# A hybrid decoder layer on one core: mixers and attention of different quarters alternate piece by piece, and the gate and value products of the last pair are taken in turn

## The chip, the cores and the metric

The kernel runs on one core of a Trainium2 chip. The metric is device time in microseconds from launch to end, lower is better; the time before is the median of three runs. Work is spread over TensorE (PE, matrix products and transposes into PSUM), VectorE (DVE), ScalarE (ACT) and the DMA queue that SyncE (SP) issues. GpSimd (POOL) makes an identity matrix and nothing else.

## The reference

One layer with 2048 tokens of width 1024, in float32:

```python
h = rms_norm(x, mix_norm_g)
lru_x, lru_gate, conf_a, conf_b = split(h @ w_in, 4)           # 512 columns each
lru_x = causal_dwconv(lru_x, lru_conv_w, lru_conv_b)           # 4 taps
y_lru = rg_lru(lru_x, ...) * gelu(lru_gate)                    # two 64x64 gates a head, a scan over time
c = causal_dwconv(conf_a * sigmoid(conf_b), conf_conv_w, ...)  # 31 taps
c = silu(layer_norm(c, ...))
x = x + concat([y_lru, c]) @ w_out
q = rms_norm(x) @ w_q;  k, v = split(rms_norm(mem) @ w_kv, 2)  # 256 memory tokens, 4 heads
x = x + softmax(q k^T / 16) v @ w_o
g, u = split(rms_norm(x) @ w_up, 2)                            # 3072 columns each
x = x + (gelu(causal_dwconv(g, 3 taps)) * u) @ w_down
return rms_norm(x, final_norm_g)
```

## The kernel before

**Arithmetic.** Each matrix product is made of three matmuls: both operands are split into a rounded high part and a low part (`split`: ScalarE copies the high part, VectorE subtracts it), and high x high, high x low and low x high are summed in PSUM (`mm3`). A weight of the mixers that was split once is kept in device memory (`Kept`) and is fetched in two parts for the other three quarters. The memory side of the attention is folded into two matrices of 1024 x 1024 beforehand: `memory_a` makes A (q and k together), `memory_vo` makes VO (v and w_o).

**Stages.** Tokens come in four quarters of 512. For each quarter q there are three tasks. `mixer(q)` (tasks `m`): norm, transpose, then `conf` (two steps, each a projection pair for conf_b and conf_a, followed by 31 taps of convolution on VectorE for two blocks) and `lru` (two steps, each a projection, 4 taps, two gates, a scan, another projection). A mixer starts when the mixer before it has ended. `normed(q)` (tasks `n`): the layer norm of the convolved half, with two column sums on TensorE. `attend(q)` (tasks `a`): `project_tokens` three times (w_out, A, VO) with transposes and a softmax between them, then the norm for the feed-forward, transposed and stored. `project` and `project_tokens` give way (`yield`) after every 12 matmuls. `first_tokens` is the first quarter's own beginning, with the first weight columns.

The feed-forward (`up`) has two halves of 1024 tokens (h = 0, 1). It goes through 12 pairs of column blocks (j); each pair has a gate product and a value product, each by Strassen's scheme with seven products of half size (`strassen_cols`). The operands of x that these need (`HalfX`: seven keys, four tiles each, high and low) stay in SBUF for a whole half: five keys of the first half are made early (`first_x`), two in the first pair. During the value product of the last pair, `used(key)` makes the second half's operand as soon as the first half's has been read. `prepare_down` makes and stores the operands of the down projection in the background. `Down` then does the down projection in three chunks for each half, and `finish` the last norm.

**Order.** The program is written as tasks (generators). `drive` keeps a clock that is the sum of TensorE's planned work; it steps the first task in the list that is due, and `yield n` makes a task due n us later on that clock (`yield task` waits for another task's end). Where none is due the clock jumps, so a wait only orders, it puts no idle time into the program. The list's order is `TURNS`. Every operation recorded this way gets a due time from its place in the order; a planner then simulates the engines, with list scheduling by due times, slots of SBUF tiles (84 of tag S of 512 columns, 4 of tag W for raw weights, 3 of tag D) and 8 PSUM banks, three passes over, and writes out the instructions in the order of the best pass. Each engine then works through its own list in order. All instructions are issued from one helper, so nearly all have line 393 in the profile; one goes by tile names: `conv` are the taps of the long convolution, `xc` those of the short one, `xh`/`xl` high and low parts of mixer inputs and gates' inputs, `yh` of the mixers' results, `xah` and `pth` operands of attention, `Xh` and `wh` the feed-forward's, `hidh` the down projection's.

The constants that set the order stand together:

```python
    EARLY, VO_WAIT, V_LATE, Z_COPIED = 5, 0, 500, ()
    MIX_WAIT, MIX_TURN, LN_SUM, LN_SQ, GATES = (0, 0, 0, 0), 8, 2, 6, 5
    MEM_WAIT, VO_LATE, ATT_TURN, FFN_TURN, X_PACE, T_PACE = 2, 0, 2, 6, 20, 10
    NORMED = [lambda: ([m[0]], 40), lambda: ([attended[0]], 90), lambda: ([attended[1]], 90), lambda: ([m[3], n[2]], 55)]
    TURNS = lambda: [later, m[0], mem_a, m[1], n[0], a[0], mem_vo, n[1], m[2], a[1], n[2], m[3], n[3], first_t, first, a[2], a[3], tail]
```

By tile names the profile shows TensorE in the first mixer to about 121 us, in `memory_a` to 178, in the second mixer to 297, in attention 0 (with the rest of `memory_vo`) to 472, in the third mixer to 571, in attention 1 to 716, in the fourth mixer to 817, in attentions 2 and 3 to 1106, in the first half of `up` to about 1570, the second to about 2010, and in the down projection to the end.

Of the kernel before, what the change touches and what calls it, by code (L numbers as in the profile page):

```python
# [17 lines left out]
P = 128  # L18
# [112 lines left out]
class Program:  # L131
# [68 lines left out]

    def dma(self, out, in_, reads=(), writes=(), join=False):
# [8 lines left out]
        o.store = bool(rd)  # L210
        self.touch(o, rd + list(reads), wr + list(writes), join)
# [21 lines left out]
    def deadlines(self, order):  # L233

        t = 0.0
        for o in self.ops:
            o.due, o.start, o.at = 1e9, None, 0.0
        for o in order:
            if o.eng == "PE":
                o.due = o.turn = t  # L240
                t += o.cost
            elif o.store:
                o.due = t + 30
# [173 lines left out]
def hybrid_layer(  # L417
# [41 lines left out]
    def ps():  # L459
        return pr.new("ps", name="ps")  # L460
# [170 lines left out]
    class Columns:  # L631


        def __init__(self, w, name, n, uses):
            self.w, self.kept, self.uses = w, Kept(name, n * 4) if uses > 1 else None, uses
            self.seen = {}

        def get(self, c0, kq):
            key = (c0, kq)
            n = self.seen[key] = self.seen.get(key, 0) + 1  # L640
            base = ((c0 // (2 * P)) * 2 + kq) * 4
            if n > 1:
                return [tuple(self.kept.get(base + 2 * f + i, (P, KQ, P), "w" + "hl"[i]) for i in range(2)) for f in range(2)]
            got = self.rounded(c0, kq, self.fetch(c0, kq))
            if n < self.uses:
                self.store(c0, kq, got)
            return got
# [34 lines left out]

    def project(W, c0, X):
        pp = [ps(), ps()]
        for kq in range(2):
            ww = W.get(c0, kq)
            for f in range(2):
                wh, wl = ww[f]
                with together():
                    for k in range(KQ):  # L690
                        x = X[kq * KQ + k]
                        mm3(pp[f][:], wh[:, k, :], wl[:, k, :], x[0][:], x[1][:], kq + k == 0, kq == 1 and k == KQ - 1)
                if kq + f < 2:
                    yield 0
        return pp


    def project_tokens(L, W, done, rest=None):

        for half in range(2):  # L700
            pt = [ps() for _ in range(NTB)]
            for k2 in range(NK // 2):
                if rest and half == 0 and k2 == NK // 4:
                    rest()
                ww = [W.get(2 * k2 + j, half) for j in range(2)]
# [58 lines left out]

    def conf(X, C, pb, row):
        for c in (0, 2):
            if pb is None:
                pb = yield from project(W_in, 3 * DL + c * P, X)
            sg = []
# [5 lines left out]
            yield 0  # L775
            pa = yield from project(W_in, 2 * DL + c * P, X)
            cbs = []
# [45 lines left out]

    def lru(q, X, L, row):
        for c in (0, 2):
            pz = yield from project(W_in, c * P, X)
            H = []
            for j in range(2):
                w = vec["v512"][:, c + j, :]
                zt = ztail[c + j]  # L830
                xc, z = tmp("xc"), scaled("z", pz[j], row)
                ACT(xc[:], z[:], AF.Identity, scale=w[:, I_LCW + 3 : I_LCW + 4], bias=w[:, I_LCB : I_LCB + 1])
                if q in Z_COPIED:
                    z = tmp("z")
                    ACT(z[:], pz[j][:], AF.Copy)
                for s in range(1, LK):
                    wt = w[:, I_LCW + 3 - s : I_LCW + 4 - s]
                    V("scalar_tensor_tensor", xc[:, s:], z[:, : TT - s], wt, xc[:, s:], op0=ALU.mult, op1=ALU.add)
                    V("scalar_tensor_tensor", xc[:, :s], zt[:, LK - 1 - s :], wt, xc[:, :s], op0=ALU.mult, op1=ALU.add)
                V("tensor_copy", zt[:], z[:, TT - LK + 1 :])  # L840
                H.append(xc)
            yield GATES
            for j in range(2):
# [26 lines left out]
                H[j] = r  # L870
            pg = yield from project(W_in, DL + c * P, X)
            for j in range(2):
# [181 lines left out]
    def mixer(q, after):  # L1054
        if after:
            yield after
            yield MIX_WAIT[q]
        if q == 0:
            X, pb, row = yield from first_tokens()
        else:  # L1060
            X, pb, row = (yield from mix_norm(q)), None, None
        C, L = [], []
        yield from conf(X, C, pb, row)
        yield from lru(q, X, L, row)
        del X, row
        mixed[q] = C, L

    def first_tokens():
# [100 lines left out]
    def attend(q, ready):  # L1169
# [10 lines left out]

        yield from project_tokens(L + Y, W_out, add)
        del L, Y
# [18 lines left out]

        yield from project_tokens(X, A_rows, soft)
        del X
# [10 lines left out]

        yield from project_tokens(PT, VO_rows, add2, lambda: turn_p(prob[1], PT))
        attended[q].done = True
# [10 lines left out]
        del xs  # L1227
        yield FFN_TURN

# [131 lines left out]
    def up(h, B, used=None):  # L1361
        for j in range(NCH):
            gb = []

# [8 lines left out]

            yield from strassen_cols(2 * j * P, B, gate)
            cvs = []
            for i in range(2):
# [9 lines left out]
            gb = None  # L1386

            def gated(f, th, a, p):
                t = tmp("up")
                V("tensor_tensor", t[:], a[:], p[:], op=ALU.add)  # L1390
                o = th * TT
                V("tensor_tensor", cvs[f][:, o : o + TT], cvs[f][:, o : o + TT], t[:], op=ALU.mult)
# [13 lines left out]
    def wd_at(c, key, i):  # L1406
        return ((c * 7 + ORDER.index(key)) * KD + i) * 2

    def prepare_down():
# [124 lines left out]
    def finish(h, acc):  # L1534
# [45 lines left out]
    NORMED = [lambda: ([m[0]], 40), lambda: ([attended[0]], 90), lambda: ([attended[1]], 90), lambda: ([m[3], n[2]], 55)]  # L1580
    ATTEND = [lambda: [n[0]], lambda: [n[1]], lambda: [n[2]], lambda: [n[3], attended[2]]]
    TURNS = lambda: [later, m[0], mem_a, m[1], n[0], a[0], mem_vo, n[1], m[2], a[1], n[2], m[3], n[3], first_t, first, a[2], a[3], tail]
    X = [HalfX(h) for h in range(NH)]
# [69 lines left out]
```

## Time and profile before

| | |
|---|---|
| median of three runs | 2496.95 us (2496.62 to 2499.46) |
| the profiled execution | 2498.48 us |
| its span, first to last instruction | 2496.7 us |
| TensorE busy, matmuls | 2466.2 us (99%), 11212 |
| VectorE busy, instructions | 1821.8 us (73%), 3041 |
| ScalarE busy, instructions | 1172.3 us (47%), 2039 |
| moved by DMA | 543.70 MB, 218 GB/s |
| mean granted TensorE clock | 0.995 |

A matmul's own duration on record is longer than the distance to the next one, since matmuls overlap; where TensorE loses time is read from idle time in short stretches, from the number of matmuls in them and from the granted clock. In the answers by stretch each row has, behind the length, busy time and (x) instructions of each engine, then the granted clock as a share of full speed, the share of the DMA engines' time, and GB/s.

### The profile page before, as it was taken

To read this page: it belongs to the slowest core of one execution; us is meant where nothing else is said; L and a number is where in the kernel's file an instruction comes from. 1 tells how busy PE (TensorE), PEld (TensorE's weight loads), DVE (VectorE), ACT (ScalarE), POOL (GpSimd) and SP (SyncE) were. 2 spreads that over 40 slices of the span, in tenths; PEclk is the share of its full clock that TensorE was granted. 3 is DMA by queue.
4 is the path that set the end of the run, shared out by engine and by line. 5 is a ranking of instruction groups with operands and counts; after the bars stand their busy time and mean duration, and the time that the engine had idled before them with its cause. 6 is when DMAs were issued, how large, how long until landed. Compare 5 with 4: busy or idle time off the path is not lost. (4 is left out here: it accounts for less than half of the span.)

```text
span 2496.7 us, 32736 instructions
## 1 busy us (share of the span) xinstructions
PE 2466.2 (99%) x11212; PEld 2042.8 (82%) x11212; DVE 1821.8 (73%) x3041; ACT 1172.3 (47%) x2039; POOL 0.7 (0%) x6
## 2 busy tenths in 40 slices
PE   9999999999999999999999999999999999999998
PEld 7897788887888788888888888788888888888887
DVE  6999974199329962339888787987866775667666
ACT  6671846336544653446455455654543432224223
POOL 0000000000000000000000000000000000000000
PEclk9999999999999999999999999999999999999999
DMA  8687676848463788557654545655422288779775
GB/s 311 208 287 267 214 262 226 317 141 298 158 243 115 245 300 316 185 194 261 237 196 149 183 161 186 237 166 181 142 75 93 69 285 284 254 237 341 257 253 177
DMA packets 327742, 543.70 MB, mean 218 GB/s; under 512 B 31581, under 2 KB 109405, under 8 KB 327575
## 3 DMA queue, kind: packets, MB, share of 16 engines
q1 hardware_dynamic: 327574, 541.60, 63.1%
q8 instruction: 89, 1.46, 0.2%
q14 instruction: 79, 0.64, 0.1%
HBM read 396.78 MB, written 144.70 MB: 217 GB/s over the span
## 5 line engine op out<-in xcount | busy, mean ns | idle before, releaser
L393 PE MATMUL ps<-Xh,wl 128*128 128x512 f32 x1344 | 523.6, 390 | 2.7 <-DVE wl L393 2.7
L393 PE MATMUL ps<-Xh,wh 128*128 128x512 f32 x1344 | 523.6, 390 | 1.8 <-ACT u L393 1.1
L393 PE MATMUL ps<-Xl,wh 128*128 128x512 f32 x1344 | 522.9, 389 | 0.0
L393 DVE SCALAR_TENSOR_TENSOR conv<-cb,v,conv 128x512 f32<-128x512 f32 x480 | 334.7, 745 | 1.9 <-ACT conv L393 1.3
L393 PEld LDWEIGHTS ps<-Xh,wl 128*128 128x128 f32 x1344 | 252.2, 188 | 57.7 <-DVE wl L393 5.3
L393 PEld LDWEIGHTS ps<-Xh,wh 128*128 128x128 f32 x1344 | 252.3, 188 | 55.9 <-ACT wh L393 1.9
L393 PEld LDWEIGHTS ps<-Xl,wh 128*128 128x128 f32 x1344 | 252.3, 188 | 52.1
L393 PE MATMUL ps<-wh,hidl 128*128 128x512 f32 x672 | 261.5, 389 | 0.4 <-DVE hidl L393 0.4
L393 PE MATMUL ps<-wh,hidh 128*128 128x512 f32 x672 | 261.5, 389 | 0.0
L393 PE MATMUL ps<-wl,hidh 128*128 128x512 f32 x672 | 261.4, 389 | 0.0
L393 DVE TENSOR_TENSOR acc<-acc,ps 128x512 f32<-128x512 f32 x192 | 129.6, 685 | 147.0 <-PE ps L393 146.5
L393 PE MATMUL ps<-xh,wh 128*128 128x512 f32 x512 | 202.7, 396 | 2.0 <-ACT xh L393 2.0
L393 PE MATMUL ps<-xl,wh 128*128 128x512 f32 x512 | 200.5, 392 | 0.3 <-DVE xl L393 0.3
L393 PE MATMUL ps<-xh,wl 128*128 128x512 f32 x512 | 200.4, 391 | 0.0
L393 ACT ACTIVATE wh<-s 128x512 fp32r<-128x512 f32 x192 | 119.6, 628 | 133.5 <-DVE s L393 98.4
L393 DVE TENSOR_TENSOR wl<-raw,wh 128x512 fp32r<-128x512 f32 x208 | 140.6, 684 | 40.5 <-ACT wh L393 33.8
L393 ACT ACTIVATE wh<-raw 128x512 fp32r<-128x512 f32 x208 | 126.9, 628 | 79.3 <-PE ps L393 43.1
L393 DVE TENSOR_TENSOR wl<-s,wh 128x512 fp32r<-128x512 f32 x192 | 131.2, 686 | 45.1 <-ACT wh L393 30.7
L393 ACT ACTIVATE u<-ps 128x512 f32<-128x512 f32 x144 | 85.9, 597 | 144.3 <-PE ps L393 142.6
L393 PEld LDWEIGHTS ps<-wh,hidh 128*128 128x128 f32 x672 | 126.1, 188 | 26.8 <-ACT hidh L393 0.4
L393 PEld LDWEIGHTS ps<-wh,hidl 128*128 128x128 f32 x672 | 126.1, 188 | 26.7 <-DVE hidl L393 0.8
L393 PEld LDWEIGHTS ps<-wl,hidh 128*128 128x128 f32 x672 | 126.2, 188 | 26.2
(205 smaller groups left out, 4264.4 us busy)
## 6 DMA issues: line engine op xcount, KB each, us to landing
raw<-in_w_up_dram SPq DMA_DIRECT2D x96, 512.0 KB
wh<-w_down SPq DMA_DIRECT2D x164, 256.0 KB
wl<-w_down SPq DMA_DIRECT2D x164, 256.0 KB
wh<-w_in SPq DMA_DIRECT2D x96, 256.0 KB
wl<-w_in SPq DMA_DIRECT2D x96, 256.0 KB
hid<-cv SPq DMA_DIRECT2D x48, 512.0 KB
h<-hid SPq DMA_DIRECT2D x96, 256.0 KB
w_down<-wh SPq DMA_DIRECT2D x84, 256.0 KB
```

What stands on the lines that cost most here:

```text
L393: getattr(e, name)(*[resolve(a) for a in args], **{k: resolve(a) for k, a in kw.items()})
```

## The change

Pieces of a mixer give way for `MIX_PACE[q]` us of the planned clock, and pieces of the three products of an attention for `ATT_PACE[q]`, where both gave way for 0 before. `TURNS`, the waits of `normed` and most other constants are different; `FFN_TURN` has a value for each quarter. In the last pair of each half of `up` the gate's and value's seven products are stepped in turn, and the value's results are held until the gate's are ready. `prepare_down` stops while the first half is in its last two pairs and the second in its first. `first_tokens` fetches both halves of the weight columns at 2*DL (conf_a) right behind those at 3*DL, ahead of the small vectors of `setup_later`. In the second quarter `lru` copies z out of PSUM by ScalarE before the taps. `finish` of the first half multiplies in place. (`dma` gains a parameter whose default is the constant used before.)

```diff
-    def project(W, c0, X):
+    def project(W, c0, X, pace=0):
...
                 if kq + f < 2:
-                    yield 0
+                    yield pace
...
-    def project_tokens(L, W, done, rest=None):
+    def project_tokens(L, W, done, rest=None, pace=0):
...
                     if tb % 2 and k2 < NK // 2 - 1:
-                        yield 0
+                        yield pace
...
-            got = self.rounded(c0, kq, self.fetch(c0, kq))
+            st = self.early.pop(key, None) or raw_cols(self.w, c0, kq)
+            got = self.rounded(c0, kq, st)
...
-                if q in Z_COPIED:
+                if row is None and q in Z_COPIED:
                     z = tmp("z")
                     ACT(z[:], pz[j][:], AF.Copy)
...
             raw.append(W_in.fetch(3 * DL, half))
+        for kq in range(2):
+            W_in.early[2 * DL, kq] = raw_cols(w_in[0], 2 * DL, kq)
...
-        yield from project_tokens(L + Y, W_out, add)
+        yield from project_tokens(L + Y, W_out, add, None, ATT_PACE[q][0])
...
-        yield FFN_TURN
+        yield FFN_TURN[q]
...
-            yield from strassen_cols(2 * j * P, B, gate)
-            cvs = []
+            def gated(f, th, a, p):
+                t = tmp("up")
+                V("tensor_tensor", t[:], a[:], p[:], op=ALU.add)
+                held.append((f, th * TT, t))
+                if cvs:
+                    multiply()
+            def multiply():
+                for f, o, t in held:
+                    V("tensor_tensor", cvs[f][:, o : o + TT], cvs[f][:, o : o + TT], t[:], op=ALU.mult)
+                held.clear()
+            parts = [strassen_cols(2 * j * P, B, gate), strassen_cols(DFF + 2 * j * P, B, gated, used if j == NCH - 1 else None)]
+            turning.done = j >= NCH - PAUSE
+            turned_over.done = h > 0 and j >= 1
+            if used and j == NCH - 1:
+                for _ in zip(*parts):
+                    yield 0
+            yield from parts[0]
...
-            yield from strassen_cols(DFF + 2 * j * P, B, gated, used if j == NCH - 1 else None)
+            multiply()
+            yield from parts[1]
...
     def prepare_down():
         yield attends[NQ - 1]
         for c in range(NCK):
             for i in range(KD):
+                if turning.done:
+                    yield turned_over
...
-                early = tmp("fin")
+                early = tmp("fin") if h else acc[th, tb, 0]
...
-    EARLY, VO_WAIT, V_LATE, Z_COPIED = 5, 0, 500, ()
-    MIX_WAIT, MIX_TURN, LN_SUM, LN_SQ, GATES = (0, 0, 0, 0), 8, 2, 6, 5
-    MEM_WAIT, VO_LATE, ATT_TURN, FFN_TURN, X_PACE, T_PACE = 2, 0, 2, 6, 20, 10
+    EARLY, VO_WAIT, V_LATE, Z_COPIED = 5, 2, 500, (0, 1)
+    MIX_WAIT, MIX_TURN, LN_SUM, LN_SQ, GATES = (0, 10, 0, 0), 9, 2, 0, 4
+    MIX_PACE, ATT_PACE = (1, 4, 4, 4), ((0, 4, 1), (0, 2, 6), (0, 1, 0), (0, 2, 4))
+    PAUSE = 2
+    MEM_WAIT, VO_LATE, ATT_TURN, FFN_TURN, X_PACE, T_PACE = 12, 10, 1, (6, 16, 6, 100), 10, 11
...
+    NORMED = [lambda: ([m[0]], 105), lambda: ([attended[0]], 35), lambda: ([attended[1]], 140), lambda: ([m[3], n[2]], 115)]
+    TURNS = lambda: [later, n[2], m[0], mem_a, m[1], n[1], n[3], a[0], n[0], mem_vo, m[2], first, a[3], a[2], a[1], m[3], first_t, tail]
```

More of the change, by code (lines that the diff above doesn't have):

```diff
@@ L199, in do, with dma @@
         self.touch(o, [r.buf for r in ins] + list(reads), [r.buf for r in outs] + list(writes))
-    def dma(self, out, in_, reads=(), writes=(), join=False):
+    def dma(self, out, in_, reads=(), writes=(), join=False, slack=30):
         o = self.op("SP")
@@ L209, in dma @@
         wr = [out.buf] if isinstance(out, Ref) else []
-        o.store = bool(rd)
+        o.store = slack if rd else False
         self.touch(o, rd + list(reads), wr + list(writes), join)
@@ L242, in deadlines @@
             elif o.store:
-                o.due = t + 30
+                o.due = t + o.store
         for o in reversed(self.ops):
@@ L635, in __init__ @@
             self.w, self.kept, self.uses = w, Kept(name, n * 4) if uses > 1 else None, uses
-            self.seen = {}
+            self.seen, self.early = {}, {}
         def get(self, c0, kq):
@@ L763, in scaled, with conf @@
         return t
-    def conf(X, C, pb, row):
+    def conf(X, C, pb, row, pace):
         for c in (0, 2):
             if pb is None:
-                pb = yield from project(W_in, 3 * DL + c * P, X)
+                pb = yield from project(W_in, 3 * DL + c * P, X, pace)
             sg = []
@@ L775, in conf @@
             yield 0
-            pa = yield from project(W_in, 2 * DL + c * P, X)
+            pa = yield from project(W_in, 2 * DL + c * P, X, pace)
             cbs = []
@@ L822, in conf_out, with lru @@
             Y.append((hi, lo))
-    def lru(q, X, L, row):
+    def lru(q, X, L, row, pace):
         for c in (0, 2):
-            pz = yield from project(W_in, c * P, X)
+            pz = yield from project(W_in, c * P, X, pace)
             H = []
@@ L870, in lru @@
                 H[j] = r
-            pg = yield from project(W_in, DL + c * P, X)
+            pg = yield from project(W_in, DL + c * P, X, pace)
             for j in range(2):
@@ L1062, in mixer @@
         C, L = [], []
-        yield from conf(X, C, pb, row)
-        yield from lru(q, X, L, row)
+        yield from conf(X, C, pb, row, MIX_PACE[q])
+        yield from lru(q, X, L, row, MIX_PACE[q])
         del X, row
@@ L1200, in soft @@
             prob[half].append(softmax(p, rp[:, tb : tb + 1], rn[:, tb : tb + 1]))
-        yield from project_tokens(X, A_rows, soft)
+        yield from project_tokens(X, A_rows, soft, None, ATT_PACE[q][1])
         del X
@@ L1213, in add2 @@
             x2_kept.put((q * NTB + tb) * 2 + half, xs[tb][half][:])
-        yield from project_tokens(PT, VO_rows, add2, lambda: turn_p(prob[1], PT))
+        yield from project_tokens(PT, VO_rows, add2, lambda: turn_p(prob[1], PT), ATT_PACE[q][2])
         attended[q].done = True
@@ L1362, in up @@
         for j in range(NCH):
-            gb = []
+            gb, cvs, held = [], [], []
             def gate(f, th, a, p):
@@ L1386, in up @@
             gb = None
[L1388 to L1392, printed above, removed]
-            yield from strassen_cols(DFF + 2 * j * P, B, gated, used if j == NCH - 1 else None)
+            multiply()
+            yield from parts[1]
             for i in range(2):
@@ L1407, in wd_at @@
         return ((c * 7 + ORDER.index(key)) * KD + i) * 2
+    turning, turned_over = Task(None), Task(None)
     def prepare_down():
@@ L1574, in setup_later @@
         vec["v3072"] = columns([ffn_conv_w[0], ffn_conv_b], DFF, "v3072")
-    EARLY, VO_WAIT, V_LATE, Z_COPIED = 5, 0, 500, ()
-    MIX_WAIT, MIX_TURN, LN_SUM, LN_SQ, GATES = (0, 0, 0, 0), 8, 2, 6, 5
-    MEM_WAIT, VO_LATE, ATT_TURN, FFN_TURN, X_PACE, T_PACE = 2, 0, 2, 6, 20, 10
-    NORMED = [lambda: ([m[0]], 40), lambda: ([attended[0]], 90), lambda: ([attended[1]], 90), lambda: ([m[3], n[2]], 55)]
+    EARLY, VO_WAIT, V_LATE, Z_COPIED = 5, 2, 500, (0, 1)
[4 more added lines that the diff above has]
+    NORMED = [lambda: ([m[0]], 105), lambda: ([attended[0]], 35), lambda: ([attended[1]], 140), lambda: ([m[3], n[2]], 115)]
     ATTEND = [lambda: [n[0]], lambda: [n[1]], lambda: [n[2]], lambda: [n[3], attended[2]]]
-    TURNS = lambda: [later, m[0], mem_a, m[1], n[0], a[0], mem_vo, n[1], m[2], a[1], n[2], m[3], n[3], first_t, first, a[2], a[3], tail]
+    TURNS = lambda: [later, n[2], m[0], mem_a, m[1], n[1], n[3], a[0], n[0], mem_vo, m[2], first, a[3], a[2], a[1], m[3], first_t, tail]
     X = [HalfX(h) for h in range(NH)]
```

## The prediction

> **What bounds the kernel now.** I read the busy line of the page first, then the costliest groups of TensorE, then busy times by stretch with cuts at the stretches where TensorE stops, then the waits and the timeline inside these.
>
> ```profile
> PE 2466.2 (99%) x11212; PEld 2042.8 (82%) x11212; DVE 1821.8 (73%) x3041; ACT 1172.3 (47%) x2039; POOL 0.7 (0%) x6
> ...
> L393 PE MATMUL ps<-Xl,wh 128*128 128x512 f32 x1344 | 522.9, 389 | 0.0
> ```
>
> ```profile
> core 0: us, PE busy (x) PEld busy (x) DVE busy (x) ACT busy (x) POOL busy (x), PEclk, DMA share, GB/s
> 0.00:30.00 30.00, 24.30 (x129) 21.18 (x130) 13.90 (x36) 17.15 (x37) 0.70 (x6) 0.94 0.69 230
> 30.00:180.00 150.00, 150.00 (x809) 130.62 (x808) 146.70 (x273) 104.69 (x182) 0.00 (x0) 1.00 0.80 272
> 180.00:240.00 60.00, 59.67 (x273) 49.10 (x272) 59.50 (x95) 12.77 (x19) 0.00 (x0) 1.00 0.89 308
> 240.00:260.00 20.00, 15.11 (x53) 11.49 (x52) 20.00 (x39) 12.16 (x18) 0.00 (x0) 0.83 0.28 102
> 260.00:290.00 30.00, 30.00 (x133) 24.86 (x132) 28.82 (x56) 19.46 (x28) 0.00 (x0) 1.00 0.44 148
> 290.00:300.00 10.00, 8.91 (x38) 6.70 (x37) 10.00 (x16) 9.90 (x15) 0.00 (x0) 1.00 0.88 305
> 300.00:560.00 260.00, 259.72 (x1226) 216.55 (x1227) 162.16 (x285) 127.03 (x245) 0.00 (x0) 1.00 0.69 243
> 560.00:600.00 40.00, 36.99 (x152) 28.79 (x151) 40.00 (x65) 31.54 (x41) 0.00 (x0) 0.96 0.85 303
> 600.00:800.00 200.00, 199.82 (x943) 166.38 (x942) 114.31 (x206) 89.68 (x183) 0.00 (x0) 1.00 0.55 189
> 800.00:850.00 50.00, 47.03 (x189) 36.85 (x188) 49.28 (x79) 34.29 (x45) 0.00 (x0) 0.93 0.73 259
> 850.00:1105.00 255.00, 254.79 (x1199) 211.62 (x1198) 118.55 (x217) 109.42 (x250) 0.00 (x0) 1.00 0.70 240
> 1105.00:1140.00 35.00, 33.17 (x161) 26.98 (x160) 24.92 (x43) 27.35 (x51) 0.00 (x0) 1.00 0.84 299
> 1140.00:1555.00 415.00, 415.00 (x1833) 343.63 (x1832) 350.41 (x560) 210.32 (x320) 0.00 (x0) 1.00 0.56 188
> 1555.00:1585.00 30.00, 27.35 (x114) 20.47 (x113) 29.54 (x47) 23.68 (x41) 0.00 (x0) 1.00 0.85 287
> 1585.00:2010.00 425.00, 425.00 (x1876) 351.89 (x1875) 327.99 (x499) 196.77 (x297) 0.00 (x0) 1.00 0.39 131
> ...
> 2290.00:2300.00 10.00, 9.58 (x42) 7.29 (x41) 8.91 (x15) 3.72 (x6) 0.00 (x0) 1.00 1.05 389
> ...
> 2490.00:2497.00 7.00, 0.00 (x0) 0.00 (x0) 2.40 (x6) 2.26 (x6) 0.00 (x0) 0.78 0.53 199
> ```
>
> TensorE sets the time. One matmul is on record for 389 ns, but in 1140 to 1555 there are 1833 of them in 415 us: one starts every 226.4 ns, so they overlap, and that spacing is the pace to beat. The change removes no matmul. All it can win is the time in which TensorE stops or runs at a lowered clock. I price a stretch as its length less busy time, plus length times the missing share of the clock: 0 to 30 loses 5.7 + 1.8 = 7.5 us; 240 to 260 loses 4.9 + 3.4 = 8.3; 290 to 300, 1.1; 560 to 600, 3.0 + 1.6 = 4.6; 800 to 850, 3.0 + 3.5 = 6.5; the rest of 180 to 1105 about 1.0 together; 2290 to 2300, 0.4; the end 6.7. In the long runs of equal matmuls I go by the count instead: 1555 to 1585 holds 114 where 30 us at 226.4 ns hold 132.5, so 18.5 x 0.2264 = 4.2 us are lost; 1105 to 1140 by busy time 1.8, and about 2.3 when a matmul that waits overlaps its neighbour as there. Together 42.6 us, and that is the ceiling.
>
> A busy share would hide part of this. The Trainium skill, in "Perfetto Trace Analysis", section Identifying the Most-Contended Engine, calls matmul busy time a poor measure of the distance to roofline because matmuls are pipelined. The rows bear it out: busy time gives 30 - 27.35 = 2.65 us for 1555 to 1585, the count 4.2; by busy time alone my sum below would be some 1.5 us smaller.
>
> Where TensorE stops between 240 and 850, VectorE is full: 58.8 of 60 us in 240 to 300, 40.0 of 40 in 560 to 600, 49.3 of 50 in 800 to 850. Between these it is at 62%, 57% and 46%. The mixers bring VectorE more than TensorE leaves time for, attention less, and the kernel runs them one after the other.
>
> ```profile
> L393 DVE SCALAR_TENSOR_TENSOR conv<-cb,v,conv 128x512 f32<-128x512 f32 x480 | 334.7, 745 | 1.9 <-ACT conv L393 1.3
> ...
> 240.40 0.74 DVE L393 SCALAR_TENSOR_TENSOR xc<-ps,v,xc 128x511 f32<-128x511 f32 x1
> 241.06 0.73 DVE L393 SCALAR_TENSOR_TENSOR conv<-cb,v,conv 128x512 f32<-128x512 f32 x1
> ...
> 246.99 0.73 DVE L393 SCALAR_TENSOR_TENSOR xc<-ps,v,xc 128x509 f32<-128x509 f32 x1
> ...
> 247.83 0.74 PE L393 MATMUL ps<-xh,gwah 128*128 128x512 f32 x1 [4.43 <-ACT xh L393]
> ```
>
> The last four lines show one such stop: VectorE works through the short convolution (xc) that the gates need in turn with taps of the long one (conv), and the gate matmul starts 4.43 us late.
>
> **The change part by part, by the places where time is lost.**
>
> *Start.* Both halves of the second weight column are now fetched ahead of the small vectors.
>
> ```profile
> 3.41 0.98 PE L393 MATMUL ps<-ident,raw 4*128 4x4 f32 x8 [3.41 <-DMA raw<-in_ffn_norm_g_dram]
> ...
> 7.45 0.58 SPq L393 DMA_DIRECT2D raw<-in_conf_conv_w_dram  x1
> ...
> 16.63 0.22 SPq L393 DMA_DIRECT2D raw<-in_conf_ln_b_dram  x1
> ...
> 18.48 0.56 SPq L393 DMA_DIRECT2D raw<-in_w_in_dram  x1
> ...
> 22.77 0.63 ACT L393 ACTIVATE wh<-raw 128x512 fp32r<-128x512 f32 x1 [4.13 <-DMA raw<-in_w_in_dram]
> ...
> 39.69 0.82 ACT L393 ACTIVATE conv<-cb,v 128x512 f32<-128x512 f32 x1 [1.84 <-DVE cb L393]
> ```
>
> The weight is issued at 18.48 behind the vectors (7.45 to 16.63) and the gate matrices, ScalarE stands 4.13 us for it, and the splits of x that TensorE needs are queued behind that instruction. Issued near 7.5 it lands by 12 (18.48 to 22.77 is 4.3 us). Of the 7.5 us, 3.4 precede the first matmul and stay; I take 3.5 of the other 4.1. Late next are the vectors: they need a slot of tag W (four), free when the first column has been split, near 12, then some 9 us on SP's queue (7.45 to 16.63), so they are there by about 24; their first user is at 39.69, 15 us of cover. Bounds: 0 to 4.1 won.
>
> *Mixers against attention.* What is moved is order: each projection piece of 12 matmuls (2.7 us) gives way for 1 us (first quarter) or 4 us, and attention's loops give way in turn; with the new order of tasks the memory's products alternate with the first mixer, `memory_vo` with the second, attention 0 with the end of the second and the third, attention 1 with the fourth. Instructions and transfers on SP stay as many; they come in another order. VectorE in 30 to 1105 sums to 749 us of 1075, 70%; conv alone is 334.7/4 = 84 us in a quarter. A mixer holds 8 x 48 + 48 matmuls, 98 us of TensorE, and an estimated 130 of VectorE (conv, and what the 146.7 us in 30 to 180 hold beside it). An attention holds 3 x 192 and 96 transposes, some 141 us; a stretch of nothing else shows VectorE at 24%, so 34 us:
>
> ```profile
> 650.00:700.00 50.00, 49.82 (x234) 41.05 (x233) 11.95 (x25) 16.90 (x46) 0.00 (x0) 1.00 0.48 170
> ```
>
> Mixed, 164 us of VectorE stand against 239, 69%. So the stops at 560 to 600 and 800 to 850 (11.1 us) should nearly go: 2 left, for the chain of the layer norm. In 30 to 300 two mixers still come early and VectorE stays full (265.0 us of 270 by its five rows); only `memory_vo` moves ahead as filler, and the first attention's output projection comes beside the second mixer's end. Of 9.4 us I leave 4. Small ones stay at 1.0. Won: 21.5 - 7 = 14.5. Bounds: 21.5 won, all of it; the other end is below nothing, the third rival. I sit nearer the gain because the rows just named leave VectorE 38 to 54% idle beside each stop.
>
> *The clock.* Half of the 240 stop's price is the clock (0.83 of 20 us); it goes with the wait. The 1.1 us stop at 290 kept 1.00.
>
> *Entry to the feed-forward.* The last quarter's 32 transposes and eight ScalarE copies wait 100 us instead of 6, and x is prepared at pace 10 instead of 20, ahead of attention 2 and 3. Of 2.3 us I leave 1.3, won 1.0; bounds 0 and 2.3. With these the weights' preparation for the down projection starts 100 us later and pauses over the last two pairs and the first of the second half (3 x 38 us). It is paced (84 steps of 8 us), so it ends near 2005 instead of 1800; its last third is not read before about 2150. VectorE has 97 us free in 1585 to 2010 for it. Cost 0, up to 2 if it collides with the start of the down products.
>
> *Last pair.* Gate and value products alternate, so each operand of x is used twice before its successor is split.
>
> ```profile
> L393 DVE TENSOR_TENSOR wl<-s,wh 128x512 fp32r<-128x512 f32 x192 | 131.2, 686 | 45.1 <-ACT wh L393 30.7 <-PE ps L393 13.1
> L393 DVE SCALAR_TENSOR_TENSOR cv<-gb,v,cv 128x1024 f32<-128x1024 f32 x96 | 122.8, 1279 | 1.8 <-ACT cv L393 1.1
> ```
>
> Before: the value half holds 84 matmuls, 19.0 us, and 4 combinations, 7 weight splits, 8 adds and multiplies and 28 splits of the next x on VectorE: 47 x 0.69 = 32.4 us, 13.4 too many, and 4 x 1.28 of convolution from the gate. After: 62 x 0.69 = 42.8 us against 38.0, 4.8 too many, the convolution behind it, and the background preparation paused. Of 4.2 us I leave 1.0; won 3.2, bounds 0 and 4.2. All eight PSUM banks and all four W slots are now held by the two products, so the next pair's weights start late; that is the 1.0.
>
> *The rest.* In the second quarter four pieces of z are copied by ScalarE: 4 x 0.6 us, hidden (ScalarE has 12.77 us busy in 180 to 240); uncovered, 2.4. `finish` of the first half multiplies in place: no instruction more, a wait for the square before it, hidden by products; the 0.4 us at 2290 stays. The end stays. DMA slack keeps its 30.
>
> Sum: 3.5 + 14.5 + 1.0 + 3.2 = 22.2 us. The profiled execution took 2498.48 for a span of 2496.7; the median is 2496.95. 2498.5 - 22.2 = 2476.3 in that execution's terms, and 1.5 less against the median: **2475**.
>
> **The rivals.**
>
> *Late chains stay.* ScalarE has 77 of its 80 table loads before 1106.
>
> ```profile
> L393 ACT ACT_TABLE_LOAD x80 | 102.6, 1283 | 47.9 <-DVE small L393 21.7 <-issue 16.7 <-PE ps L393 7.5
> ...
> L393 ACT ACT_TABLE_LOAD x30 | 38.5, 1283 | 8.7 <-PE ps L393 7.5 <-PEq L1639 0.7
> ...
> L393 ACT ACT_TABLE_LOAD x47 | 60.3, 1283 | 39.1 <-DVE small L393 21.7 <-issue 16.7
> ```
>
> (all; 0 to 350; 350 to 1106.)
>
> Alternating sigmoid, gelu and square root of a mixer with the exponentials of attention could double them: 77 x (1.28 + 0.60 idle) = 145 us more on ScalarE, which sums to 568 us in the 1105; 65% then. On average that is no bound, but the gate chain passes three tables, and each load in it delays VectorE's next work. For it: ScalarE is at 79% in 560 to 600 already. If half of the 14.5 us is lost again, 2482; if nearly all, 2489. I say 2485, chance 0.16. The rule behind it is in the Trainium skill, "ScalarE: Activation LUTs", section Table sets: the hidden batching unit: batch activations by set. That page also puts a drain of 1380 ns to each load, where this trace shows 0.6 us of idle on the mean.
>
> *No effect where it counts.* VectorE's work is the same 749 us, and the full stretch just moves: mixing wins nothing or loses a few, start and last pair give 0 to 6.7. About 2494, chance 0.12.
>
> *Slower: tiles run out.* Program text: 84 S tiles. Mixer 2 beside attention 0 holds 16 (x) + 12 (its results) + 12 (results of mixer 1) + 4 (gates), attention 8 + 16: 68, where a mixer alone had some 52. The remaining 16 serve temporaries and two streams of weights, 4 tiles a set, a set lasting 24 matmuls, 5.4 us, against 4.3 us to fetch one (1.05 MB at the 243 GB/s of 300 to 560). Without a spare set each wait falls on TensorE and lowers the clock as at 240. With 48 mixer sets in the three alternating quarters, 22.2/48 = 0.46 us a set undoes the whole gain. One in six waiting the full 4.3 costs 34: 2475 + 34 = 2509. Against it: of TensorE's waits one alone names a transfer, at the very start, and the DMA share is 0.55 to 0.70 in 300 to 560, 600 to 800 and 850 to 1105.
>
> ```profile
> PE ps L393 <- DMA raw<-in_ffn_norm_g_dram: 3.4, 1, 3.4
> ```
>
> Chance 0.14.
>
> **How the numbers follow.** The forecast has 0.58, with 2467 to 2483 of its own (all bounded gains together, or half of the mixing's). 0.2%, 5 us, is about what a measurement of this kernel can tell from no change. Faster: 0.58 + 0.16 = 0.74; within: 0.12; slower: 0.14. The range 2465 to 2499 leaves out the third rival and a little below.
>
> **What would show it.** Right: a third `raw<-in_w_in` issued before the small vectors and a clock near 1.00 up to 30; no stretch between 300 and 850 with VectorE full and TensorE under 99%; some 222 matmuls in every 50 us about 1570. Wrong: TensorE waiting for `wh` or `wl` from DMA while mixer and attention alternate; more than 120 table loads; a new gap at the layer norm sums or near 2010.

## The result, and the profile after

The changed kernel takes 2471.47 us (median of four runs, 2469.63 to 2473.47) against 2497.05 of the kernel before; the ratio is 0.9896, 95% interval 0.9879 to 0.9913. The forecast was 2475 (2465 to 2499). The profiled execution has a span of 2471.6 us, 25.1 less.

The busy line after, and ScalarE's table loads of the whole span:

```profile
PE 2453.0 (99%) x11212; PEld 2040.1 (83%) x11212; DVE 1826.1 (74%) x3041; ACT 1171.3 (47%) x2041; POOL 0.7 (0%) x6
```

```profile
L394 ACT ACT_TABLE_LOAD x78 | 100.1, 1283 | 49.8 <-DVE small L394 32.9 <-issue 14.8 <-PEq L1661 0.7
```

TensorE's and VectorE's instructions are the same in number as before, and VectorE and ScalarE are busy as long within 5 us. Busy times by stretch after, columns as in the answer shown of before:

```profile
0.00:30.00 30.00, 26.69 (x149) 23.71 (x150) 15.14 (x38) 17.38 (x37) 0.70 (x6) 1.00 0.76 238
30.00:180.00 150.00, 146.11 (x775) 127.05 (x774) 143.26 (x267) 102.28 (x180) 0.00 (x0) 0.99 0.80 275
240.00:260.00 20.00, 20.00 (x91) 16.78 (x90) 20.00 (x34) 2.40 (x4) 0.00 (x0) 1.00 0.37 117
290.00:300.00 10.00, 10.00 (x46) 8.32 (x45) 10.00 (x13) 9.88 (x12) 0.00 (x0) 1.00 0.83 309
560.00:600.00 40.00, 40.00 (x178) 33.14 (x177) 36.74 (x65) 26.13 (x37) 0.00 (x0) 1.00 0.77 254
800.00:850.00 50.00, 47.95 (x208) 38.53 (x207) 35.54 (x56) 30.25 (x49) 0.00 (x0) 1.00 0.89 319
1540.00:1570.00 30.00, 30.00 (x134) 24.86 (x133) 29.69 (x49) 18.00 (x30) 0.00 (x0) 1.00 0.38 124
```

Three of the four stops between 240 and 850 us are gone, the fourth is down to 2.05 us, and the change of halves (1540 to 1570) runs without a gap. The second mixer's gates, which start at 247.8 us before and at 276.9 after, show it best: VectorE is as full around them as it was, and TensorE does not stop. A new loss stands in 30 to 180.

```profile
250.00:285.00 35.00, 35.00 (x155) 28.88 (x154) 35.00 (x64) 15.07 (x24) 0.00 (x0) 1.00 0.58 198
```

Where the 25.1 us came from is read best from stretches that hold the same work in both kernels, cut at the same places of the program: from the second mixer's first transposes to the feed-forward's first product; from there over the first pair; from the last pair of the first half to the second pair of the second half. The first stretch is shown for the kernel before and for the changed one, then the other two for the kernel before, and for the changed one:

```profile
178.80:1106.40 927.60, 914.62 (x4209) 754.67 (x4208) 604.51 (x1053) 447.93 (x842) 0.00 (x0) 0.99 0.67 233
```

```profile
180.60:1089.00 908.40, 904.10 (x4209) 750.60 (x4208) 605.46 (x1047) 448.62 (x844) 0.00 (x0) 1.00 0.69 236
```

```profile
1106.50:1150.80 44.30, 42.47 (x201) 34.72 (x200) 35.03 (x59) 35.13 (x61) 0.00 (x0) 1.00 0.80 282
1531.60:1612.40 80.80, 78.15 (x337) 62.49 (x336) 72.25 (x116) 49.88 (x83) 0.00 (x0) 1.00 0.69 233
```

```profile
1089.10:1131.70 42.60, 42.45 (x201) 34.70 (x200) 35.02 (x58) 34.39 (x58) 0.00 (x0) 1.00 0.77 259
1512.50:1588.70 76.20, 76.20 (x338) 63.09 (x337) 69.14 (x109) 45.11 (x74) 0.00 (x0) 1.00 0.54 179
```

The bracket behind TensorE's busy time shows the same 4209 matmuls taking 927.6 and 908.4 us: 19.2 won. The first pair gives 1.7, the change of halves 4.6. The first stretch, up to the second mixer, ends at 178.8 before and at 180.6 after: 1.8 lost. What follows the change of halves gives the last 1.4 (2496.7 - 1612.4 = 884.3, and 2471.6 - 1588.7 = 882.9). -1.8 + 19.2 + 1.7 + 4.6 + 1.4 = 25.1. How far one profile can be trusted is seen from runs below that issue the same instructions up to the feed-forward: the stretch of 927.6 us took 927.5 in `b_pair`, and that of 908.4 took 908.8 in `a_noturn` and 908.6 in `a_nopause`. The first stretch scatters more, as is said below.

The order itself can be counted by TensorE's tiles. In the stretch of 4209 matmuls the kernel before changes 5 times between a mixer's projections and gates (`xh`, `xl`) and an attention's products (`yh`, `xah`, `pth` and their low parts): each mixer and each attention runs in one piece. The changed kernel changes 71 times.

The new loss, in the waits of TensorE up to 179 us and the stretch around the second of them:

```profile
PE ps L394 <- DMA raw<-in_w_kv_dram: 2.4, 1, 2.4
PE ps L394 <- ACT mem L394: 1.5, 1, 1.5
```

```profile
140.00:160.00 20.00, 17.63 (x103) 15.92 (x102) 17.94 (x31) 11.40 (x28) 0.00 (x0) 0.91 0.94 307
```

With the start's stop gone, TensorE comes to the memory's transposes near 51 us before ScalarE has scaled them, and to a weight of `memory_a` at 149 us before its transfer has landed (the DMA share is 0.94 there); the granted clock is 0.91 in this stretch, where the kernel before has 1.00.

### The profile page after: what moved, and what is told of

Its sections match the earlier page's. It is cut to its first block, busy times and chain, and to the rows that moved or that the text cites. A ratio compares the mean times of both kernels' runs of the same rounds, so it can differ in the third digit from the quotient of the medians.

```text
span 2471.6 us, 32772 instructions
## 1 busy us (share of the span) xinstructions
PE 2453.0 (99%) x11212; PEld 2040.1 (83%) x11212; DVE 1826.1 (74%) x3041; ACT 1171.3 (47%) x2041; POOL 0.7 (0%) x6
```

## The experiments

All ratios are to the kernel before, timed beside the run; where a size is read from stretches, both ends are the same places of the program as above.

**The early fetch alone, and all but the early fetch.** `b_early` is the kernel before with

```diff
+        for kq in range(2):
+            W_in.early[2 * DL, kq] = raw_cols(w_in[0], 2 * DL, kq)
```

and the lines that take it up. 

> The kernel before with the early fetch of the second weight column alone. Both theories: the third weight transfer is issued near 7.5 us and ScalarE no longer stands 4.1 us for it; the stop of TensorE near 21 us is gone. Theory 'given back' (in the changed kernel the second mixer's first transposes start at 180.6 us against 178.8 before, though the start has no stop any more: TensorE comes earlier to weights of memory_a that a transfer brings at the same time as before): the second mixer's transposes still start within 1 us of 178.8, and the time is 2497 +- 2. Rival 'lost to the new order' (the loss in memory_a comes from the changed waits of its tasks, not from the earlier start): the transposes start at 174 to 175.5 and the time is 2492 to 2494.

Measured: ratio 0.9996 (0.9987 to 1.0006). `a_noearly` is the changed kernel without these lines. 

> The changed kernel without the early fetch. Theory 'given back': the stop near 21 us returns (2 to 4 us), the waits near 50 and 149 us shrink by as much, the second mixer's transposes start within 1 us of 180.6, and the time is 2471.5 +- 2. Rival 'lost to the new order': the stop near 21 us comes on top, the transposes start at 183 to 185, the time is 2474 to 2476.

Measured: 2473.72 us, ratio 0.9904 (0.9889 to 0.9918), where the changed kernel has 0.9896. The fetch does what it says: in 15 to 35 us TensorE starts 101 matmuls in `b_early` and 104 in the changed kernel, against 83 in the kernel before and 84 in `a_noearly`. TensorE waits for other things then. Its waits up to 179 us, behind that of 3.3 or 3.4 us for the first transfer, `b_early` first, `a_noearly` second:

```profile
PE ps L393 <- ACT mem L393: 1.8, 1, 1.8
```

```profile
PE ps L394 <- DMA raw<-in_w_kv_dram: 2.3, 1, 2.3
PE ps L394 <- ACT xh L394: 2.0, 1, 2.0
PE ps L394 <- DVE xl L394: 0.3, 1, 0.3
PE ps L394 <- DMA x<-in_x_dram: 0.2, 1, 0.2
```

The wait for `mem` comes with the early fetch: it stands in every profile of a kernel that has the fetch (0.4 to 2.7 us) and in none without, so a part of what the fetch wins is given back at once. The wait for the memory's weight stands in `a_noearly` too, so the fetch is not what brings it. Nor is it shown to be the changed order: of the eight profiles with the changed constants four have it (0.9 to 2.4 us) and three stop there for something else, by 1.1 to 1.2; `before`, `b_early` and `b_pair` don't stop there, but `b_taps`, `b_notab` and `b_both` below, which keep the old order, wait 0.8 to 1.1 us for that weight.

What both theories said of the second mixer's start could not be settled: it lies at 176.0 in `b_early`, at 181.2 in `a_noearly`, but also at 176.5 in `b_pair` below, whose program is the kernel before up to the feed-forward, and at 176.9 in `a_nopause` and 177.6 in `a_noturn`, whose program is the changed one up to there. One profile of the first 180 us is good to 2 to 4 us and no better, so the 1.8 us lost above are not shown. By the medians the fetch is worth 1 us in the old kernel (0.9996) and 2 in the changed one (0.9904 against 0.9896), and neither is clear of nothing.

**The paces.** `a_nopace`, and then one side alone (`a_mixonly`, `a_attonly`):

```diff
-    MIX_PACE, ATT_PACE = (1, 4, 4, 4), ((0, 4, 1), (0, 2, 6), (0, 1, 0), (0, 2, 4))
+    MIX_PACE, ATT_PACE = (0, 0, 0, 0), ((0, 0, 0),) * 4                              # a_nopace
+    MIX_PACE, ATT_PACE = (1, 4, 4, 4), ((0, 0, 0),) * 4                              # a_mixonly
+    MIX_PACE, ATT_PACE = (0, 0, 0, 0), ((0, 4, 1), (0, 2, 6), (0, 1, 0), (0, 2, 4))  # a_attonly
```

> The changed kernel with all paces of mixers and attention at 0, the order of tasks and all other constants kept. Theory 'alternation relieves VectorE': without paces mixers and attention run one after the other, VectorE is full (98% or more) again for 40 us or more around the gates and layer norms after 300 us, TensorE stops there, and 10 to 15 of the 19 us won between the second mixer's start and the feed-forward go: 2482 to 2487. Rival 'the order of tasks and their waits do it': the paces are worth under 4 us, 2471 to 2475.

> The changed kernel with the attention's paces at 0 and the mixers' paces kept. With all paces at 0 the time was 2507.7. Theory 'the mixer must give way, and attention as well': an attention without paces keeps TensorE for itself once it runs, since it stands ahead of the next mixer in the list, so mixers 3 and 4 run in one piece behind it; half or more of the 36 us stays lost, 2488 to 2504. Rival 'giving way on the mixers' side is enough': 2471 to 2477.

> The changed kernel with the mixers' paces at 0 and the attention's paces kept. A mixer that starts in a gap of an attention then keeps TensorE until its own explicit waits, so it runs nearly in one piece. Theory 'both must give way': 2488 to 2508. Rival 'the attention's paces are what counts': 2471 to 2477.

Measured: 2507.74 (1.0042, 1.0025 to 1.0059), 2484.89 (0.9956, 0.9941 to 0.9970) and 2496.95 (1.0004, 0.9995 to 1.0013). Without paces the new constants are slower than the kernel before, so the order of tasks and their waits alone win nothing; I had expected 10 to 15 us lost, it is 36. With the attention's paces at 0 the time lies between what the two theories of `a_mixonly` gave; with the mixers' paces at 0 the theory that both must give way holds. The two stretches, `a_nopace`, `a_mixonly`, `a_attonly` in turn; in the first two, where 16 transposes and a wait stand between the last attention's products and the first pair, they are cut ahead of these:

```profile
178.40:1114.60 936.20, 915.54 (x4208) 755.18 (x4207) 599.17 (x1042) 430.17 (x828) 0.00 (x0) 0.99 0.66 230
1114.60:1166.80 52.20, 45.44 (x202) 37.28 (x201) 43.37 (x73) 40.71 (x68) 0.00 (x0) 0.90 0.76 260
```

```profile
178.20:1091.50 913.30, 907.57 (x4209) 751.34 (x4207) 598.12 (x1040) 448.27 (x841) 0.00 (x0) 1.00 0.68 235
1091.50:1142.50 51.00, 44.25 (x202) 36.38 (x201) 43.33 (x73) 40.41 (x68) 0.00 (x0) 0.93 0.75 266
```

```profile
176.80:1112.10 935.30, 913.44 (x4209) 754.30 (x4208) 606.34 (x1049) 432.48 (x833) 0.00 (x0) 0.99 0.67 230
1112.20:1154.80 42.60, 42.46 (x201) 34.71 (x200) 35.02 (x58) 34.42 (x58) 0.00 (x0) 1.00 0.78 259
```

The two sides do different things. The mixers' paces make the gain of the mixing stage: 936.2 falls to 913.3 with them alone, and stays at 935.3 with the attention's alone; both give 908.4. TensorE changes between mixer and attention 9 times without paces, 47 times with the mixers' alone and 33 with the attention's alone. So it is not the number of changes that counts: with the attention's paces alone the second mixer still runs in one piece (408 matmuls), and it is there that work beside the gates is missing.

The attention's paces make the entry to the feed-forward: 42.6 us with them, 51 to 52 without. There TensorE stands 6.3 us for the norm of the last attention's tokens (`xn`), in `a_mixonly` and `a_nopace` alike, and the clock is 0.93 and 0.90 over the stretch:

```profile
PE ps L394 <- ACT xn L394: 6.3, 1, 6.3
```

VectorE has 73 instructions in the first pair instead of 58, since it is still splitting the operands of x beside that norm. The likely reason, read from the code and not tried alone: `first_x` runs by planned time, paces with nothing else ready let that time jump, and without them the last attention is over before the operands' turn comes.

**Which engine's load makes the stops.** Three forms of the kernel before, one run each, all without a new order: TensorE changes between mixer and attention 5 times in each, after the same numbers of matmuls as in the kernel before. `b_taps` leaves out 16 of the 30 VectorE taps; `b_notab` replaces the square root of `lru` and of `wide_rstd`, the gelu and the silu by copies of the same size (one of four such lines is shown); `b_both` does both.

```diff
-                for t in range(1, CK):
+                for t in range(1, CK // 2):
```

```diff
-                ACT(m[:], m[:], AF.Sqrt, scale=-1.0)
+                ACT(m[:], m[:], AF.Copy, scale=-1.0)
```

> The kernel before with 14 of the 30 VectorE taps of the long convolution; the other 16 are left out, 256 instructions of 0.70 us, 179 us of VectorE. It puts the disputed cause to the test without any new order. Theory 'VectorE is full there': TensorE's stops near 243, 298, 582 and 836 us (20.5 us with their clock) fall to 5 or less, and the time goes to about 2481. Rival 'the stops are the length of the chains from gate and norm to the next product': they stay over 12 us, time over 2488.

> The kernel before, all its taps kept, but with the square root, the gelu and the silu of mixers and layer norm left out (copies of the same size stand in their place), so that ScalarE has some 35 table loads fewer there. Theory 'the stop near 836 us is ScalarE's table loads' (with half the taps left out it stayed, 8.5 us; ScalarE is full around it, 11 loads in 28 us): that stop falls from 6.5 us to under 2, those near 243 and 298 stay at 7 or more together, and the time falls by 4 to 7 us. Rival 'the chain of the layer norm is too long for the work that covers it, loads or not': over 4 us stay near 836.

> The kernel before with both left out: 16 of 30 taps, and the functions that need tables. Theory 'VectorE at the first three stops, ScalarE's loads at the fourth': of the 20.5 us between 240 and 850 at most 5 stay. Rival 'too little other work for TensorE beside gates and norms, whatever the engines' load': 8 or more stay, the gates' stop near 243 above all (it kept 5 us without the taps).

The four stops, in `b_taps`, `b_notab` and `b_both`:

```profile
240.00:260.00 20.00, 17.01 (x67) 13.37 (x67) 19.31 (x39) 14.51 (x20) 0.00 (x0) 0.91 0.30 110
290.00:300.00 10.00, 10.00 (x44) 8.00 (x43) 7.32 (x7) 9.94 (x16) 0.00 (x0) 1.00 0.87 289
560.00:600.00 40.00, 40.00 (x174) 32.23 (x173) 23.82 (x34) 27.39 (x42) 0.00 (x0) 1.00 0.95 342
800.00:850.00 50.00, 45.69 (x183) 35.70 (x182) 28.35 (x43) 33.40 (x48) 0.00 (x0) 0.93 0.79 270
```

```profile
240.00:260.00 20.00, 15.25 (x54) 11.63 (x53) 20.00 (x40) 13.09 (x18) 0.00 (x0) 0.83 0.25 95
290.00:300.00 10.00, 10.00 (x44) 7.85 (x43) 10.00 (x16) 8.22 (x15) 0.00 (x0) 1.00 0.95 313
560.00:600.00 40.00, 39.24 (x165) 30.90 (x166) 40.00 (x63) 23.49 (x38) 0.00 (x0) 1.00 0.94 340
800.00:850.00 50.00, 48.04 (x205) 37.77 (x204) 50.00 (x80) 26.16 (x42) 0.00 (x0) 1.00 0.78 273
```

```profile
240.00:260.00 20.00, 17.00 (x67) 13.33 (x66) 18.71 (x37) 14.98 (x22) 0.00 (x0) 0.91 0.32 119
290.00:300.00 10.00, 10.00 (x44) 8.01 (x43) 9.32 (x11) 7.75 (x15) 0.00 (x0) 1.00 0.93 300
560.00:600.00 40.00, 40.00 (x176) 32.77 (x175) 22.01 (x30) 16.40 (x32) 0.00 (x0) 1.00 0.90 321
800.00:850.00 50.00, 49.88 (x227) 40.88 (x226) 28.21 (x40) 20.70 (x42) 0.00 (x0) 1.00 0.78 275
```

VectorE is no longer full in `b_taps` at 800 to 850 (28.35 of 50 us), and TensorE still loses 4.3 us and 7% of the clock. Without the functions that stop falls to 2.0 us and keeps its clock, though VectorE is full (50.0). What TensorE waited for at 836 was `yh`, the layer norm's result, in the kernel before, `b_taps` and `b_notab`:

```profile
PE ps L393 <- ACT yh L393: 2.5, 1, 2.5
PE ps L393 <- ACT yh L393: 3.3, 1, 3.3
PE ps L393 <- ACT yh L393: 0.6, 2, 0.5
```

The copies take ScalarE as long as the functions did (gelu 598 and 592 ns on the mean, the square root of `lru` 627 and 625), but its table loads fall from 80 to 46. So the stop at 836 is that of ScalarE's loads; the one at 582 goes without the taps and nearly goes without the functions; the one at 290 goes with either. At 243 the taps are worth 3.5 of 8.3 us, and 4.8 stay in `b_both`. VectorE is still busy for 18.71 of 20 us there, with the taps that are left. That these 4.8 us are the chain from the projection to the gates, with too little other work for TensorE beside it, is therefore argued and not shown. What is shown is that a new order takes them away: in the changed kernel TensorE waits for no `xh` between 180 and 1090 us. The whole stage in these three:

```profile
179.60:1097.50 917.90, 910.20 (x4209) 753.18 (x4208) 466.36 (x829) 444.19 (x839) 0.00 (x0) 0.99 0.68 234
179.10:1098.70 919.60, 910.33 (x4209) 751.62 (x4208) 602.66 (x1050) 414.06 (x816) 0.00 (x0) 1.00 0.67 234
177.20:1086.50 909.30, 905.50 (x4209) 751.67 (x4208) 466.39 (x829) 407.39 (x810) 0.00 (x0) 1.00 0.68 237
```

The same 4209 matmuls take 917.9, 919.6 and 909.3 us, so the taps left out are worth 9.7 us, the functions 8.0, and both together 18.3 of 927.6 - nearly what the change won by order alone, with every tap and function in place. Against what was expected: `b_taps` kept 12.6 us of the stops (4.8 and 7.8) and took 2489.98 us, so its first theory falls and the rival's figures hold. `b_notab` did what its first theory said (2.0 us left at 836, 8.2 at 243 and 298, 2491.76 us beside 2495.81). `b_both` left 4.9 us, nearly all of it at the gates, and took 2477.11; that is under the 5 of its first theory, and the rival named the right place. Of the 8.0 us some 2 may be chance: `b_early`, with the same mixers, loses 3.5 us at the fourth stop as well but no clock (see the end), and took 925.6 us for the stage.

What ScalarE does at the fourth stop of the kernel before, its table loads in 28 us and the busy times of that stretch:

```profile
L393 ACT ACT_TABLE_LOAD x11 | 14.1, 1283 | 0.2
```

```profile
810.00:838.00 28.00, 26.20 (x114) 20.99 (x112) 28.00 (x42) 27.68 (x35) 0.00 (x0) 1.00 1.02 368
```

Half of ScalarE's 27.68 busy us are loads of tables, between the last gates of the fourth mixer and a layer norm that TensorE waits for. The Trainium skill, "ScalarE: Activation LUTs", section Table sets: the hidden batching unit, asks to batch activations by set; `b_notab` gives a size for what is at stake here: without 25 of the stage's 60 loads it is 8.0 us shorter.

**The last pair.** `b_pair` is the kernel before with `up` and `prepare_down` of the change; `a_noturn` leaves the loop over `zip(*parts)` out of the changed kernel, `a_nopause` has `PAUSE = 0`.

> The kernel before with the last pair's products in turn and the pause of prepare_down, nothing else. My working: 3 to 5 us won between the start of the first half's last pair and the second pair of the second half, none elsewhere: 2492 to 2494. Rival (the entry changes and the later preparation do it): 0 to 1 us there, 2496 to 2497.

> The changed kernel with the last pair's gate and value products one after the other, the pause of prepare_down kept. Theory 'each operand used twice gives VectorE the time': the stop at the change of halves returns by 2 to 4 us, all of it between the start of the last pair and the second pair of the second half: 2474 to 2476. Rival 'the pause alone frees VectorE': under 1 us, 2471 to 2472.5.

> The changed kernel without the pause of prepare_down; gate and value of the last pair in turn as in the change. Without the turns but with the pause the stretch from the last pair to the second pair of the second half took 78.4 us, with both 76.2, before the change 80.8. Theory 'two halves of one relief': 77.5 to 79 us in this stretch, time 2472 to 2475. Rival 'the turns alone are enough': 76.2 to 76.8 us, 2471 to 2472.

Measured: 2491.38 (0.9977, 0.9968 to 0.9986), 2474.46 (0.9916, 0.9900 to 0.9933), 2477.51 (0.9926, 0.9909 to 0.9942). The stretch over the change of halves in the three:

```profile
1529.10:1605.30 76.20, 76.20 (x337) 63.08 (x337) 69.11 (x109) 44.96 (x74) 0.00 (x0) 1.00 0.53 179
```

```profile
1509.80:1588.20 78.40, 77.02 (x337) 62.83 (x336) 68.42 (x109) 46.44 (x75) 0.00 (x0) 1.00 0.53 178
```

```profile
1508.90:1592.50 83.60, 80.41 (x337) 64.79 (x336) 74.07 (x118) 49.37 (x81) 0.00 (x0) 0.96 0.64 214
```

By itself the edit wins in the old kernel what it wins in the new one: 80.8 to 76.2 us. The changed kernel with the pause and without the turns has 2.4 of the 4.6. The turns without the pause give nothing: 83.6 us, more than before the change. VectorE then has 118 instructions there instead of 109, and the clock is 0.96. My "two halves" was wrong in that point: the turns need the pause. No run leaves both out of the changed kernel, so the 2.4 us can hold a share of its other constants, and the 83.6 as well.

**Fewer tiles.** `a_s80` is the changed kernel with `S=80` in `SLOTS` instead of 84. 

> The changed kernel with 80 tiles of tag S instead of 84. Tests how near the rival 'tiles run out' was. If tiles are what alternation lives on: four tiles less cost 6 us or more between the second mixer's start and the feed-forward, with TensorE waiting for weights there, time 2478 or more. If there is room: within 3 us of 2471.5.

Measured: 2483.53 us (0.9951, 0.9936 to 0.9965), 12 us more than with 84 by the medians and 14 by the ratios. The two stretches and the longest waits of TensorE in them:

```profile
175.60:1092.10 916.50, 908.09 (x4209) 751.76 (x4208) 604.25 (x1046) 452.01 (x843) 0.00 (x0) 1.00 0.68 234
1092.20:1140.90 48.70, 44.55 (x202) 35.81 (x202) 41.12 (x68) 37.73 (x63) 0.00 (x0) 0.96 0.71 239
```

```profile
PE ps L394 <- ACT wh L394: 3.1, 2, 1.7
PE ps L394 <- DVE yl L394: 2.3, 1, 2.3
```

The mixing stage loses 8.1 us, the entry 6.1. Tiles are scarce, but not as I had put it: TensorE waits for splits and the layer norm, and none of its waits in the two stretches names a transfer. Nothing but the number of tiles differs, so they cause it; by which tile that came free late was not followed.

## Why the prediction was right, and where it was not

*Start: 3.5 won predicted.* The stop went: 0 to 30 us lost 7.5 before and loses 3.3 now, with the clock at 1.00, and both halves of the weight are issued ahead of the small vectors. But the stretch up to the second mixer ended 1.8 us later in the profile, within its scatter. The step that failed is "late next": I named the small vectors and gave them 15 us of cover, and they were not late; late was ScalarE's scaling of the memory at 51 us, which I had left out. Behind it the profile has a wait for the memory's weight at 149, which I had at nothing; what brings it is open. By the times the term is about 1 to 2, not clear of nothing.

*Mixers against attention: 14.5 predicted, 19.2 measured.* The stops went as forecast, the layer norm left 2.05 us where I had left 2, and the first two stops went wholly where I had left 4. The reason was half right. I laid the stops to VectorE because it was full beside each of them. It was full, but the fourth stop was ScalarE's table loads, and more than half of the first stayed with 16 of 30 taps and the functions left out. What the order supplies is other work for TensorE beside all of these chains; VectorE's work in the stage is 604.5 us before and 605.5 after, and it is still full around the second mixer's gates. Also, "the memory's products alternate with the first mixer" did not happen: the first of them starts at 97.9 us, where it started at 75.9 before; which of the constants moved it was not tried.

*The clock* went with the waits, as said: 1.00 in 240 to 260.

*Entry: 1.0 predicted, 1.7 measured.* *Last pair: 3.2 predicted, 4.6 measured*; I had kept 1.0 for late weights behind the full PSUM banks, and there is no gap at all; 4.6 is a little beyond the bound of 4.2. *The rest: 0 predicted, 1.4 measured.* Of that, 0.4 is TensorE's wait for `hidl` at 2290, which I had said stays and which is gone; the other 1.0 is open.

*The sum.* 2475 against 2471.47 is closer than its terms: the start came out some 2 to 5 us below what I gave it, the mixing 4.7 above, and these nearly cancel. That part is luck. The way, the place of most of the gain and the range were not.

*The signs.* They came as named for being right but for one: in 750 to 800 VectorE is full (50.00 of 50 us) and TensorE busy for 49.16, just under 99%. None of those for being wrong came, but for 1.7 us that TensorE waits at 814 for a layer norm's sum, which the forecast had left in.

*Rivals.* Table loads did not double, they are 78 instead of 80; but loads were already behind the fourth stop of the kernel before. "No effect where it counts" fell with the 19.2 us. "Tiles run out" did not happen with 84, and `a_s80` shows that it was four tiles away from half the gain.

## What to carry to other kernels

An engine that is full beside a stop is a suspect, not the cause: take its load away, and then the other engine's, and see which stop goes; two engines can share the stops of one stage, and an engine can stay full when the stop is gone. Work laid beside a wait is worth as much as the load taken off the engine waited for (19.2 us against 18.3 here, with half the taps left out), but the edits that arrange it hang together: the changed kernel without its paces loses 36 us, more than the whole change wins, and an interleaved stretch also needs its background work held off. A single profile of this start is no measure of 2 us; time such an edit or leave it open.

## What the runs showed of the hardware

A stop of 2 to 3 us lowers the granted clock in one execution and not in another. In the changed kernel it was 0.91 over 140 to 160 us with a wait of 2.4 us at 149; in `a_noearly` it stayed at 1.00 over the same 20 us with a wait of 2.3 us. The fourth stop of the kernel before cost clock as well (0.93 over 800 to 850); `b_early`, whose mixers are the same, loses 3.5 us of busy time there and none of the clock:

```profile
800.00:850.00 50.00, 46.50 (x199) 36.81 (x198) 50.00 (x82) 34.98 (x48) 0.00 (x0) 1.00 0.77 273
```

So the share of the clock in the price of a short stop, 3.5 of 6.5 us there, is not the same in each execution, and a price read from one profile can be off by that much.
